# Two norm chains after memory attention, emitted between the gates of the second half-step

## The chip, the cores and the metric

The kernel runs on one core of one Trainium2 chip, in float32 throughout (matrix products take each operand as a high and a low float32r part). The metric is the device time of one execution in microseconds, the median of repeated runs. Before the change it was 2316.18 us (3 runs, 2313.41 to 2321.45).

## What is computed

One step of a one-layer decoder for 1,024 prompt tokens and 8 x 4 sample tokens, 1,056 tokens in all, of width 1024. The part that matters here is the end of the layer:

```python
c = memory_attend(rms_norm(h, p['xa_pre_g']), mem_k, mem_v, p['w_mem_q'], p['w_mem_o'])
h = h + rms_norm(c, p['xa_post_g'])
h = h + 0.5 * rms_norm(swiglu(rms_norm(h, p['ffn2_pre_g']), p['ffn2_w_gate'], p['ffn2_w_up'],
                              p['ffn2_w_down']), p['ffn2_post_g'])

def rms_norm(x, g):
    y = x * lax.rsqrt(jnp.mean(x * x, axis=-1, keepdims=True) + RMS_EPS)
    return y * g

def swiglu(x, w_gate, w_up, w_down):
    return (jax.nn.silu(x @ w_gate) * (x @ w_up)) @ w_down
```

`w_mem_o` is 1024 x 1024, the gate and up weights are 1024 x 2816, the down weight is 2816 x 1024.

## The kernel before

**Tiles.** The tokens are cut into three microbatches of 352 columns, t = 0, 1 and 2. An activation lies as 8 chunks of 128 features by 352 tokens. The high and low parts that TensorE reads are the tiles `X`; the raw activations lie in four large buffers, `K0` to `K3`. A product of 128 x 128 weights with 352 tokens is three matmuls (high by high, high by low, low by high, in `mm3`, L106).

**Weights.** Each block of 128 x 1024 weights is loaded by SyncE's queue into one of two `raw` buffers (L93), copied to its high part by ScalarE (L100) and subtracted into its low part by VectorE (L101). Six `w` buffers hold the split blocks, so three gates' worth of gate and up weights.

**The stage around the change.** `project(a["w_mem_o"], ...)` multiplies the attention output by `w_mem_o`, for t = 0, then 1, then 2, eight chunks of 24 matmuls each, and after each microbatch calls `after_o`. ScalarE empties each finished bank into the microbatch's `K` buffer (L1247). `after_o` then runs two norms on that buffer:

- `postnorm`: squares of the eight chunks (ScalarE, L115) are added up (VectorE, L117), one TensorE matmul with ones sums over the features (L164, into a bank `px`), VectorE takes the reciprocal root (L165, then L126 to L134), scales each chunk (L220) and adds the residual (L221). The residual comes chunk by chunk from DRAM (L1255) into two small buffers in `K1`, so chunk k+2 is not loaded before chunk k is added. The sum is stored to DRAM from ScalarE's queue (L1392, 1408 KB).
- for t = 1 and t = 2, `norm_in_place`: once more squares, sums, a matmul with ones and the reciprocal root, then eight products (L396), over the same buffer. For t = 0 it is `prenorm`, which writes `X` tiles.

**The gates.** Then 22 calls of `gate_up` run the gate and up products of t = 0 alone ("lone gates"): 24 matmuls into a gate bank and 24 into an up bank, VectorE scales the gate (L233), ScalarE takes the silu (L234), VectorE multiplies by the up bank (L235), and ScalarE's queue stores the product `sg` to DRAM (L236). There are six banks, so three gates, and two `sg` buffers. Microbatches 1 and 2 enter TensorE only after the gates and the down product of t = 0: `pair_operands` (L287 and on) reads both normed buffers and works on both at once.

**What sets the order.** The code is written in a sequence; a scheduler turns it into one fixed instruction list per engine, and gives earlier written work the higher priority. On the chip each engine walks its own list in order, and an instruction that waits holds up those behind it. DMA issues stand in the lists of SyncE and ScalarE.

Of the kernel before, what the change touches and what calls it, by code (L numbers as in the profile page):

```python
# [28 lines left out]
def decoder_step(tc, a, o):  # L29
# [18 lines left out]
    def R(tag, shape, bufs=1, dtype=F32, p=None):  # L48
        return (p or rp[0]).tile(list(shape), dtype, name=tag, tag=tag, bufs=bufs)

    def K(i):
        return kp_.tile([128, 2816], F32, name=f"K{i}", tag=f"K{i}", bufs=1)

    def K8(i):
        return K(i).rearrange("p (k n) -> p k n", n=NT)
# [12 lines left out]
    def bank():  # L68
        turn.append(turn.pop(0))
        return turn[-1].tile([128, 512], F32, name="mm", tag="mm", bufs=turn.count(turn[-1]))  # L70
# [19 lines left out]
    def stage(src, raw=None, width=1024):  # L90
        if raw is None:
            raw = wp.tile([128, 1024], F32, name="raw", tag="raw", bufs=2)[:, :width]
        sy.dma_start(raw, src)  # L93
        return raw

    def loadw(src, raw=None, width=1024):
        if raw is None:
            raw = stage(src, width=width)
        w = wp.tile([128, 2, 1024], F32R, name="w", tag="w", bufs=6)[:, :, :width]
        sc.activation(w[:, 0], raw, AF.Copy)  # L100
        v.tensor_sub(w[:, 1], raw, w[:, 0].bitcast(F32))  # L101
        return w

    def mm3(p, w, col, x, k, first, last, n=NT):
        for i, (wa, xa) in enumerate(PASSES):
            pe.matmul(p, w[:, wa, col:col + 128], x[xa][:, k, :n],  # L106
                      start=first and i == 0, stop=last and i == 2)
# [101 lines left out]
    def prenorm(t, h, gi, wide=False):  # L209
        hi, lo, tot = X(t), X(t), total()  # L210
        for k in range(8):
            half(hi, lo, h, gi, k)
            addsq(tot, h[:, k], k == 0)
        return hi, lo, (rstd_wide if wide else rstd)(tot, tag="rs", bufs=3)

    def postnorm(y, gi, resid, wide=False, last=False):
        ch = [y[:, k] for k in range(8)]
        rs = rstd_last(ch) if last else (rstd_wide if wide else rstd)(sqsum(ch))
        for k in range(8):
            v.scalar_tensor_tensor(y[:, k], y[:, k], gain(gi, k), rs, op0=ALU.mult, op1=ALU.mult)  # L220
            v.tensor_add(y[:, k], resid(k), y[:, k])  # L221
# [5 lines left out]
    def gate_up(x, w, out):  # L227
        pg, pu = bank(), bank()
        for p, ww in ((pg, w[0]), (pu, w[1])):
            for k in range(8):  # L230
                mm3(p[:, :NT], ww, k * 128, x, k, k == 0, k == 7)
        s = R("sg", [128, NT], 2)
        v.tensor_mul(s, pg[:, :NT], x[2])  # L233
        sc.activation(s, s, AF.Silu)  # L234
        v.tensor_mul(s, s, pu[:, :NT])  # L235
        sc.dma_start(out, s)  # L236

    def down(wd, h, y, parts, rs=None, filler=lambda: None):
        for c0, n in parts:
            p = [bank() if c < 6 else pbank() for c in range(n)]  # L240
            for k in range(0, NH, 2):
                x = R("raw2", [128, 1024], 2)[:, :2 * NT].rearrange("p (k n) -> p k n", k=2)
                hid = hidden(2)
                sy.dma_start(x, h[:, k:k + 2])
                split(x, hid[:, :, 0], hid[:, :, 1])
                if n == 8:
                    ws = [loadw(wd[k + j]) for j in range(2)]
                else:
                    raw = wp.tile([128, 1024], F32, name="raw", tag="raw", bufs=2)
                    for j in range(2):  # L250
                        sy.dma_start(raw[:, 512 * j:512 * j + 512], wd[k + j][:, c0 * 128:c0 * 128 + 512])
                    w = loadw(None, raw)
                    ws = [w[:, :, 0:512], w[:, :, 512:1024]]
                for j in range(2):
                    for c in range(n):
                        for q, (wa, xa) in enumerate(PASSES):
                            pe.matmul(p[c][:, :NT], ws[j][:, wa, c * 128:c * 128 + 128], hid[:, j, xa],  # L257
                                      start=k + j == 0 and q == 0, stop=k + j == NH - 1 and q == 2)
                    filler()
            for c in range(n):  # L260
                if rs is not None:
                    v.tensor_mul(y[:, c0 + c], p[c][:, :NT], rs)  # L262
                elif c % 2:
                    v.tensor_copy(y[:, c0 + c], p[c][:, :NT])
                else:
                    sc.activation(y[:, c0 + c], p[c][:, :NT], AF.Copy)
# [126 lines left out]
    def norm_in_place(y, gi):  # L393
        rs = rstd_wide(sqsum([y[:, k] for k in range(8)]))
        for k in range(8):
            v.scalar_tensor_tensor(y[:, k], y[:, k], gain(gi, k), rs, op0=ALU.mult, op1=ALU.mult)  # L396
# [384 lines left out]
    y = K8(ta)  # L781
# [17 lines left out]
    for i, t in enumerate((tb, tc_)):  # L799
        y = K8((tc_, tb)[i])  # L800
# [433 lines left out]
    def project(src, xs, order, done, before=lambda t: None, filler=lambda: None, ks=range(8)):  # L1234
        res = [loadw(src[c]) for c in range(4)]
        for t in order:
            before(t)
            y = K8(ys.pop(0))
            for c in range(8):
                w = res[c] if c < 4 else loadw(src[c])  # L1240
                p = bank()
                for k in ks:
                    mm3(p[:, :NT], w, k * 128, xs[t], k, k == ks[0], k == ks[-1])
                if len(xs[t]) == 3:
                    v.tensor_mul(y[:, c], p[:, :NT], xs[t][2])
                else:
                    sc.activation(y[:, c], p[:, :NT], AF.Copy)  # L1247
                filler()
            done(t, y)

    def resid(src):
        def get(k):
            hcs.append(hcs.pop(0))
            x = hcs[-1]
            sy.dma_start(x, src[:, k])  # L1255
            return x
        return get
# [129 lines left out]
        while t == 2 and next(sample[0], 0) is None:  # L1387
            pass

    def after_o(t, y):  # L1390
        postnorm(y, G_XA_POST, resid(hd[1][t]), True)
        sc.dma_start(hd[2][t], y)  # L1392
        if t == 0:
            xn[t] = prenorm(t, y, G_FFN2_PRE, True)
            return
        norm_in_place(y, G_FFN2_PRE)
        xn[t] = y

    project(a["w_mem_o"], cx, (0, 1, 2), after_o, drain, step)


# [16 lines left out]
    h2 = [scratch(f"h2_{t}", [128, NH, NT]) for t in range(3)]  # L1418
    for j in range(NH):
        gate_up(xn[0], (loadw(a["wg2"][j]), loadw(a["wu2"][j])), h2[2][:, j])  # L1420
    y = K8(3)
    down(a["wd2"], h2[2], y, ((0, 8),), xn[0][2])
    finish2(0, y)
# [4 lines left out]
    for i, parts in ((0, ((0, 8),)), (1, ((0, 4), (4, 4)))):  # L1428
        y = K8((3, 2)[i])
# [128 lines left out]
```

## Time and profile before

| | before |
|---|---|
| median of three runs | 2316.18 us |
| the profiled execution's own time | 2323.28 us |
| its span in the profile | 2321.5 us |
| TensorE busy with matmuls | 2233.3 us, 96% |
| VectorE busy | 1606.6 us, 69% |
| ScalarE busy | 987.1 us, 43% |
| mean granted TensorE clock | 0.981 |

The span is one execution as the hardware profiler saw it; the 1.8 us between it and the execution's own time lie outside the first and last instruction. "Busy" is the time in which an engine had an instruction running. TensorE's is the one engine near its limit, so a microsecond counts only where TensorE stands still, or runs at a lower clock. The profile's row of granted clock shows the latter: 1.00 is full speed.

### The profile page before, as it was taken

The numbers are of one execution on the slowest core, as the hardware profiler recorded it, in microseconds if no ns is written. First come the engines' busy times: TensorE is split into PE (matmuls) and PEld (weight loads), VectorE is DVE, ScalarE is ACT, GpSimd is POOL, SyncE is SP. The second block draws the span as 40 slices with busy tenths as digits, with TensorE's granted clock in tenths as the row PEclk, the third lists the DMA queues.
The fourth block names the chain that finished last, engine by engine and source line by source line (L and its number), as shares of the span: only waits on it lengthen the run. The fifth ranks groups of instructions, "written<-read, shape, count | busy, mean of one in ns | idle before, by whom it ended". The sixth has DMA issues, their size and how long they took to land.

```text
span 2321.5 us, 36671 instructions
## 1 busy us (share of the span) xinstructions
PE 2233.3 (96%) x14141; PEld 2137.7 (92%) x14141; DVE 1606.6 (69%) x3357; ACT 987.1 (43%) x1784; POOL 9.7 (0%) x22
## 2 busy tenths in 40 slices
PE   8999999999999999999899999995999999999997
PEld 8999999999999998887899789895999999999997
DVE  8986778897557658688668654687446676665474
ACT  5434345554445314356544223442334444444352
POOL 0000000000000000000000000000000000000000
PEclk9999999999999999999899999997999999999998
DMA  7567545455667323443145631454556343335673
GB/s 259 175 186 206 171 126 170 136 167 160 205 186 239 122 62 125 143 144 97 46 138 159 241 110 54 159 177 145 176 162 201 95 147 108 119 98 189 186 221 110
DMA packets 151278, 355.23 MB, mean 153 GB/s; under 512 B 17952, under 2 KB 68384, under 8 KB 149664
## 3 DMA queue, kind: packets, MB, share of 16 engines
q1 hardware_dynamic: 99712, 294.30, 41.3%
q10 hardware_dynamic: 51392, 58.59, 7.3%
q8 instruction: 111, 1.82, 0.3%
q14 instruction: 63, 0.52, 0.1%
HBM read 296.35 MB, written 59.59 MB: 153 GB/s over the span
## 4 chain that ended last, share of the span: by engine, by line
PE 81%; DVE 8%; DMA 7%; ACT 2%; issue 1%; ACTq 1%; SPq 0%; DVEq 0%
PE mm L106 26%; PE mm L333 21%; PE mm L257 14%; PE px L106 3%; PE px L257 3%; DMA sp<-K 1%; PE cs L1290 1%; DVE K L497 1%; PE cv L1315 1%; DVE w L101 1%; PE px L1212 1%; PE ac L913 1%; DVE K L220 1%; PE px L478 1%; DVE K L221 1%
## 5 line engine op out<-in xcount | busy, mean ns | idle before, releaser
L106 PE MATMUL mm<-X,w 128*128 128x352 f32 x4272 | 711.5, 326 | 12.1 <-ACT X L196 6.3
L106 PEld LDWEIGHTS mm<-X,w 128*128 128x128 f32 x4272 | 689.1, 189 | 26.7 <-issue 9.0
L100 ACT ACTIVATE w<-raw 128x1024 fp32r<-128x1024 f32 x293 | 309.1, 1056 | 387.9 <-PE mm L106 112.6
L101 DVE TENSOR_TENSOR w<-raw,w 128x1024 fp32r<-128x1024 f32 x293 | 358.3, 1223 | 163.8 <-ACT w L100 161.1
L257 PE MATMUL mm<-hid,w 128*128 128x352 f32 x2640 | 455.2, 327 | 13.8 <-DVE hid L185 7.5
L257 PEld LDWEIGHTS mm<-hid,w 128*128 128x128 f32 x2640 | 432.6, 189 | 18.2 <-DVE hid L185 10.3
L333 PE MATMUL mm<-xq,w 128*128 128x352 f32 x2112 | 364.5, 323 | 1.9 <-DVE K L262 1.3
L333 PEld LDWEIGHTS mm<-xq,w 128*128 128x128 f32 x2112 | 341.7, 188 | 4.3 <-DVE K L262 1.6
L313 DVE TENSOR_TENSOR w<-raw,w 128x512 fp32r<-128x512 f32 x308 | 202.8, 686 | 48.1 <-ACT w L312 47.0
L312 ACT ACTIVATE w<-raw 128x512 fp32r<-128x512 f32 x308 | 180.1, 624 | 119.4 <-PE mm L333 36.2
L333 PE MATMUL mm<-X,w 128*128 128x352 f32 x1056 | 186.6, 323 | 2.1 <-ACT q L347 2.1
L333 PEld LDWEIGHTS mm<-X,w 128*128 128x128 f32 x1056 | 171.2, 188 | 4.7 <-ACT q L347 3.2
L185 DVE TENSOR_TENSOR hid<-raw,hid 128x704 fp32r<-128x704 f32 x88 | 78.2, 890 | 92.3 <-ACT hid L184 87.2
L184 ACT ACTIVATE hid<-raw 128x704 fp32r<-128x704 f32 x88 | 69.5, 789 | 142.9 <-PE px L257 59.2
L497 DVE TENSOR_TENSOR K<-K 128x256 f32<-128x256 f32 (+4 forms) x380 | 105.8, 318 | 25.0 <-DMA sp<-K 12.4
L257 PE MATMUL px<-hid,w 128*128 128x352 f32 x528 | 101.9, 327 | 0.0
L117 DVE TENSOR_TENSOR tot<-tot,sq 128x352 f32<-128x352 f32 x179 | 93.1, 520 | 10.8 <-ACT sq L115 8.4
L115 ACT ACTIVATE sq<-K 128x352 f32<-128x352 f32 x170 | 80.8, 489 | 42.1 <-DVE tot L117 24.7
L333 PE MATMUL mm<-K,w 128*128 128x352 f32 x528 | 97.6, 325 | 0.0
L257 PEld LDWEIGHTS px<-hid,w 128*128 128x128 f32 x528 | 89.6, 190 | 0.0
L333 PEld LDWEIGHTS mm<-K,w 128*128 128x128 f32 x528 | 87.0, 188 | 1.1 <-issue 1.1
L1247 ACT ACTIVATE K<-mm 128x352 f32<-128x352 f32 x48 | 22.3, 465 | 86.4 <-PE mm L106 86.1
(328 smaller groups left out, 2192.2 us busy)
## 6 DMA issues: line engine op xcount, KB each, us to landing
raw<-wd SPq DMA_DIRECT2D x88, 512.0 KB
raw<-wu SPq DMA_DIRECT2D x87, 512.0 KB
raw<-wg SPq DMA_DIRECT2D x86, 512.0 KB
raw<-h SPq DMA_DIRECT2D x88, 352.0 KB
raw<-wd SPq DMA_DIRECT2D x88, 256.0 KB
h<-hid ACTq DMA_DIRECT2D x44, 352.0 KB
sp<-sp SPq DMA_DIRECT2D x16, 848.0 KB
h<-K ACTq DMA_DIRECT2D x9, 1408.0 KB
```

What stands on the lines that cost most here:

```text
L100: sc.activation(w[:, 0], raw, AF.Copy)
L101: v.tensor_sub(w[:, 1], raw, w[:, 0].bitcast(F32))
L106: pe.matmul(p, w[:, wa, col:col + 128], x[xa][:, k, :n], start=first and i == 0, stop=last and i == 2)
L115: sc.activation(q, c, AF.Square)
L117: eng.tensor_add(tot, tot, q)
L184: sc.activation(hi, x, AF.Copy)
L185: v.tensor_sub(lo, x, hi.bitcast(F32))
L257: pe.matmul(p[c][:, :NT], ws[j][:, wa, c * 128:c * 128 + 128], hid[:, j, xa], start=k + j == 0 and q == 0, stop=k + j == NH - 1 and q == 2)
L312: sc.activation(w[:, 0], x, AF.Copy)
L313: v.tensor_sub(w[:, 1], x, w[:, 0].bitcast(F32))
L333: pe.matmul(p, w[a_][:, wa, k * 128:k * 128 + 128], x[b_][xa][:, k], start=start and k == 0 and i == 0, stop=k == 3 and i == 2, skip_group ...
L497: v.tensor_tensor(out, x, y, op)
```

## The change

`after_o` keeps the norms of t = 0 where they were. For t = 1 and t = 2 it only remembers the microbatch, and the same two norms, now in `last_norm`, are called after gate 1 (for t = 1) and after gate 3 (for t = 2) of the 22 lone gates. No operation is added or left out; the lists differ in order only.

```diff
-    def after_o(t, y):
+    def last_norm(t, y):
         postnorm(y, G_XA_POST, resid(hd[1][t]), True)
         sc.dma_start(hd[2][t], y)
         if t == 0:
...
             return
         norm_in_place(y, G_FFN2_PRE)
         xn[t] = y
+
+    rest = []
+
+    def after_o(t, y):
+        if t == 0:
+            last_norm(t, y)
+        else:
+            rest.append((t, y))
 
     project(a["w_mem_o"], cx, (0, 1, 2), after_o, drain, step)
 
@@ -1418,6 +1426,8 @@
     h2 = [scratch(f"h2_{t}", [128, NH, NT]) for t in range(3)]
     for j in range(NH):
         gate_up(xn[0], (loadw(a["wg2"][j]), loadw(a["wu2"][j])), h2[2][:, j])
+        if j in (1, 3):
+            last_norm(*rest[j // 2])
     y = K8(3)
```

What it does to the lists is seen best on VectorE. In the list before, at the end of the second norm of t = 2 (`K_15049` is its buffer, `K_11753` is `K1` with the residual); the two L233 rows are those of gates 2 and 3, and the L235 row is that of gate 2:

```order
L221 TENSOR_TENSOR K_15049<-K_11753,K_15049 128x352 x2
L117 TENSOR_TENSOR tot<-tot,sq 128x352 x2
L165 TENSOR_SCALAR tot<-px 128x352
L126 TENSOR_SCALAR y<-tot 128x352
L127 SCALAR_TENSOR_TENSOR sq<-y 128x352
L128 TENSOR_TENSOR sq<-sq,tot 128x352
L129 SCALAR_TENSOR_TENSOR y<-sq,y 128x352
L233 TENSOR_TENSOR sg<-mm,rs 128x352
L130 TENSOR_TENSOR sq<-y 128x352
L233 TENSOR_TENSOR sg<-mm,rs 128x352
L131 TENSOR_TENSOR sq<-sq,tot 128x352
L235 TENSOR_TENSOR sg<-sg,mm 128x352
```

In the changed list the same gate 2 stands inside the first norm of t = 1, which begins with the L165 row; the first L235 row is that of gate 1, the L233 and the last L235 are those of gate 2:

```order
L235 TENSOR_TENSOR sg<-sg,mm 128x352
L165 TENSOR_SCALAR tot<-px 128x352
L101 TENSOR_TENSOR w<-raw,w 128x1024
L126 TENSOR_SCALAR y<-tot 128x352
L127 SCALAR_TENSOR_TENSOR sq<-y 128x352
L128 TENSOR_TENSOR sq<-sq,tot 128x352
L129 SCALAR_TENSOR_TENSOR y<-sq,y 128x352
L233 TENSOR_TENSOR sg<-mm,rs 128x352
L130 TENSOR_TENSOR sq<-y 128x352
L101 TENSOR_TENSOR w<-raw,w 128x1024
L131 TENSOR_TENSOR sq<-sq,tot 128x352
L185 TENSOR_TENSOR hid<-raw_16835,hid 128x2x352
```

Gate 2's rows have moved from behind the norms of both microbatches to ahead of nearly all of them, and from there on the L233, L235 and L101 rows of one gate after another alternate with the rows of the norms, up to gate 15.

On TensorE the matmuls with ones move. In the list before, these are the last two of them, `px_15301` (first norm of t = 2) and `px_15363` (its second); `mm_15667` is the up bank of gate 4, `mm_15731` the gate bank of gate 5, and `X0` the operand of t = 0:

```order
L164 MATMUL px_15301<-tot_15278,ones_96 128x352
L106 MATMUL mm_15667<-X0_14601,w_15663 128x352 x2
L106 MATMUL mm_15667<-X0_14602,w_15663 128x352
L106 MATMUL mm_15667<-X0_14601,w_15663 128x352 x2
L106 MATMUL mm_15667<-X0_14602,w_15663 128x352
L106 MATMUL mm_15667<-X0_14601,w_15663 128x352
L164 MATMUL px_15363<-tot_15340,ones_96 128x352
L106 MATMUL mm_15731<-X0_14601,w_15723 128x352
```

In the changed list the first matmul with ones of t = 1 stands at the end of gate 1, and its second is this one, `px_15397`, inside the up bank of gate 6 (`mm_15797`):

```order
L106 MATMUL mm_15797<-X0_14601,w_15793 128x352 x2
L106 MATMUL mm_15797<-X0_14602,w_15793 128x352
L164 MATMUL px_15397<-tot_15374,ones_96 128x352
L106 MATMUL mm_15797<-X0_14601,w_15793 128x352 x2
L106 MATMUL mm_15797<-X0_14602,w_15793 128x352
```

Where 7 gate matmuls stood between the two sums of t = 2, the changed list has 221 between those of t = 1, and 210 between those of t = 2 (from gate 9 to gate 14).

SyncE's list decides when the residual chunks are loaded. In the list before, the last six of t = 2 (`h_2`) stand together behind all weights loaded so far:

```order
L93 DMA raw<-wu 128x1024
L1255 DMA K_11753<-h_2_134 128x352 x6
L244 DMA raw_16835<-h_2_15395 128x704
```

In the changed list those of t = 1 (`h_1`) go in pairs between weight loads and a first load for the down product (L244):

```order
L1255 DMA K_11753<-h_1_133 128x352 x2
L93 DMA raw<-wg 128x1024
L93 DMA raw<-wu 128x1024
L1255 DMA K_11753<-h_1_133 128x352 x2
L93 DMA raw<-wg 128x1024
L244 DMA raw_16898<-h_2_15181 128x704
L1255 DMA K_11753<-h_1_133 128x352 x2
L93 DMA raw<-wu 128x1024
```

A pair now waits its turn behind up to two blocks of weights, and the weights behind a pair wait until two chunks have been added. On ScalarE the stores of gates 0 and 1 (L236), which stood behind the 1408 KB store of t = 2 (L1392), now follow right on their silu. Behind the last gate all lists are as they were.

## The prediction

> **What bounds the kernel now.** I read the page first: the row of busy tenths by slice (58 us each) and the row of the granted clock.
>
> ```profile
> PE   8999999999999999999899999995999999999997
> PEclk9999999999999999999899999997999999999998
> ```
>
> TensorE is full nearly everywhere. One slice stands out, the 28th (1567 to 1625 us): busy 5, clock 7. So next the busy time by stretches around it; the columns are length, then the busy time (and instructions) of each engine, the granted clock, the DMA share and GB/s.
>
> ```profile
> 1538.60:1578.50 39.90, 39.90 (x246) 39.18 (x245) 30.57 (x53) 18.63 (x27) 0.00 (x0) 1.00 0.63 205
> 1578.50:1605.40 26.90, 1.54 (x2) 0.53 (x3) 19.94 (x40) 5.13 (x10) 0.00 (x0) 0.59 0.44 147
> 1605.40:1620.00 14.60, 14.59 (x76) 14.60 (x77) 12.90 (x24) 5.25 (x8) 0.00 (x0) 0.82 0.39 98
> 1620.00:1740.00 120.00, 120.00 (x752) 120.00 (x751) 55.21 (x64) 40.61 (x49) 0.00 (x0) 1.00 0.57 173
> ```
>
> Before and behind the hole TensorE has no gap. In the hole VectorE works 19.94 of 26.90 us. TensorE's timeline says who ended the hole:
>
> ```profile
> 1554.12 22.67 PE L106 MATMUL mm<-X,w 128*128 128x352 f32 x139
> 1576.63 0.75 PE L164 MATMUL px<-tot,ones 128*128 128x352 f32 x2
> 1576.95 1.55 PE L106 MATMUL mm<-X,w 128*128 128x352 f32 x7
> 1599.97 1.54 PE L164 MATMUL px<-tot,ones 128*128 128x352 f32 x2 [21.47 <-DVE tot L117]
> 1605.41 133.18 PE L106 MATMUL mm<-X,w 128*128 128x352 f32 x816 [3.90 <-DVE sg L233]
> ```
>
> After the seven matmuls of gate 4 TensorE stands 21.47 us before the last matmul with ones (second norm of t = 2): its operand needs the whole first norm. Then 3.90 us more for a free bank, which L233 of gate 2 must empty. VectorE's and ScalarE's timelines show why gate 2 is so late:
>
> ```profile
> 1555.03 0.51 DVE L235 TENSOR_TENSOR sg<-sg,mm 128x352 f32<-128x352 f32 x1
> ...
> 1599.39 0.53 DVE L117 TENSOR_TENSOR tot<-tot,sq 128x352 f32<-128x352 f32 x1 [0.50 <-ACT sq L115]
> ...
> 1604.74 0.52 DVE L233 TENSOR_TENSOR sg<-mm,rs 128x352 f32<-128x352 f32 x1 [0.60 <-DMA h<-sg]
> ```
>
> ```profile
> 1598.49 0.33 ACTq L1392 DMA_DIRECT2D h<-K  x1
> ...
> 1598.89 1.39 ACTq L236 DMA_DIRECT2D h<-sg  x2
> ```
>
> No gate is evicted from 1555.03 (end of gate 1) to 1604.74: the rest of both norms stands ahead in VectorE's list. The stores of gates 0 and 1, which free the two `sg` buffers, are issued behind the big store at 1598.49. What ends last is thus the chain of t = 2, with gates 2 to 4 full behind it.
>
> **The change, part by part.** *The hole goes.* TensorE stops at 1578.50 and resumes at 1605.41: 26.91 us. The matmul with ones in it remains and costs, at full speed, what the spacing of ScalarE's evictions in `project` shows:
>
> ```profile
> 1519.16 0.47 ACT L1247 ACTIVATE K<-mm 128x352 f32<-128x352 f32 x1 [1.66 <-PE mm L106]
> ...
> 1523.59 0.47 ACT L1247 ACTIVATE K<-mm 128x352 f32<-128x352 f32 x1 [3.02 <-PE mm L106]
> ...
> 1527.43 0.47 ACT L1247 ACTIVATE K<-mm 128x352 f32<-128x352 f32 x1 [2.43 <-PE mm L106]
> ```
>
> A chunk of 24 matmuls takes 3.84 us (1523.59 to 1527.43), so 0.160 us each and 7.68 us a gate; with a matmul with ones in it 4.43 us, so that one costs 0.59 us. Removed: 26.91 - 0.59 = 26.3 us.
>
> *The clock stays up.* Behind the hole the clock comes back late:
>
> ```profile
> 1608.00:1610.00 2.00, 2.00 (x9) 2.00 (x8) 1.51 (x4) 0.79 (x1) 0.00 (x0) 0.50 0.45 159
> 1610.00:1612.00 2.00, 2.00 (x12) 2.00 (x11) 2.00 (x6) 0.00 (x0) 0.00 (x0) 0.85 0.33 62
> 1612.00:1614.00 2.00, 2.00 (x15) 2.00 (x14) 2.00 (x5) 0.76 (x2) 0.00 (x0) 1.00 0.30 118
> ```
>
> The 816 matmuls of gates 5 to 21 run from 1605.41 to 1738.42, where the down product's first matmul starts:
>
> ```profile
> 1738.42 2.59 PE L257 MATMUL mm<-hid,w 128*128 128x352 f32 x15
> ```
>
> That is 133.0 us; at 0.160 us they take 130.6. Without the hole 2.4 us more go.
>
> The Trainium skill ("TensorE: Matmul & The Clock Gate", Part 1) says that the array's clock falls to half after an idle window of about 3.4 us and comes back after about 3.4 us of sustained work. The granted 0.50 agrees, but it lasts here from 1605.41 to beyond 1610, some 5 us. By the Trainium skill's 3.4 us at half speed this term would be an estimated 1.7 us and the sum 28.0 us. I go by the rows.
>
> *The norms move into the gates.* Every operation remains: per microbatch two roots of 10 steps, 8 L220, 8 L221, 7 + 7 L117 and 8 L396 on VectorE, the squares on ScalarE, two matmuls with ones, eight residual loads on SyncE and a store on ScalarE's queue, of these sizes:
>
> ```profile
> h<-K ACTq DMA_DIRECT2D x2, 1408.0 KB
> K<-h SPq DMA_DIRECT2D x14, 176.0 KB
> ```
>
> The matmuls with ones are paid before and after. The rest lies beside TensorE's work if two things hold: VectorE keeps the gates fed, and each sum is ready when TensorE reaches its matmul with ones. In the steady gates VectorE is busy 55.21 of 120 us, so 4.1 of 7.68 us a gate are free. Two chains from the end of gate 1 to about gate 16 are 15 gates, so 62 us free. How long the parts take when VectorE runs without waiting:
>
> ```profile
> 1563.79 0.53 DVE L133 TENSOR_TENSOR sq<-sq,tot 128x352 f32<-128x352 f32 x1
> 1564.23 0.52 DVE L117 TENSOR_TENSOR tot<-tot,sq 128x352 f32<-128x352 f32 x1
> 1564.67 0.52 DVE L134 SCALAR_TENSOR_TENSOR y<-sq,y 128x352 f32<-128x352 f32 x1
> 1565.10 1.22 DVE L101 TENSOR_TENSOR w<-raw,w 128x1024 fp32r<-128x1024 f32 x1
> 1566.24 4.05 DVE L396 SCALAR_TENSOR_TENSOR K<-K,c_gains,y 128x352 f32<-128x352 f32 x8
> ```
>
> So 0.44 us for a small operation, 1.14 for a weight split, 4.0 for eight products; the root's steps need each other's results, and I take 0.5 for each. A microbatch is 20 x 0.5 + 22 x 0.44 + 2 x 4.0 = 27.7 us, two are 55 of 62 us. It fits, with little to spare.
>
> *The second sum.* From the first matmul with ones of t = 1 to its second TensorE has 221 matmuls, 35.4 us. VectorE's list has between them the root steps (10 x 0.5), L220 (4.0), 23 rows of L221, L117, L233 and L235 (10.1), 8 weight splits (9.1) and two L185 for the down product (some 1.6, taken at 0.8): 29.8 us. For t = 2 it is 210 matmuls, 33.6 us, against 5.0 + 4.0 + 10.1 + 7 splits at 1.14 = 27.1 us. What VectorE waited in the chain inside the hole:
>
> ```profile
> L221 DVE TENSOR_TENSOR K<-K,K 128x352 f32<-128x352 f32 x8 | 4.1, 524 | 2.8 <-DMA K<-h 2.8
> ...
> L117 DVE TENSOR_TENSOR tot<-tot,sq 128x352 f32<-128x352 f32 x7 | 3.7, 522 | 1.5 <-ACT sq L115 1.5
> ```
>
> That is 4.3 us, which leaves 1.3 us for t = 1 and 2.2 us for t = 2. A new wait on TensorE can cost nothing, or, with late residual loads, the sums of the rivals below; a gain below nothing is excluded, since TensorE has no gap in the gates (120.00 of 120.00 us). The nearest row is the chain of t = 1 as it runs before, with loads and splits interleaved and TensorE not waiting:
>
> ```profile
> 1522.60:1553.80 31.20, 31.20 (x196) 31.07 (x195) 26.48 (x44) 16.68 (x26) 0.00 (x0) 1.00 0.65 203
> ```
>
> There 193 matmuls were enough for the same chain. I take nothing.
>
> *Queues.* SyncE's 16 loads and the two stores are 16 x 176 + 2 x 1408 KB = 5.6 MB, over 15 gates (115 us) some 50 GB/s on top of 173, so about 220 GB/s, near the 203 and 205 GB/s at which TensorE had no gap. On SyncE a pair of residual loads that waits for VectorE holds the weight loads behind it, but the splits run about two gates (15 us) ahead of use. On ScalarE's queue the store of gate 5 stands behind the 1408 KB store of t = 1. In the hole such a store took 5.8 us (1598.89 to 1604.74); L233 of gate 7, which needs its buffer, comes 1.5 gates or 11.5 us later, which hides it.
>
> *What is late next.* Nothing needs the normed buffers before L287, at 1739 us:
>
> ```profile
> 1609.93 4.05 DVE L396 SCALAR_TENSOR_TENSOR K<-K,c_gains,y 128x352 f32<-128x352 f32 x8
> ...
> 1739.13 1.62 DVE L287 TENSOR_TENSOR xq<-K 128x1408 f32<-128x1408 f32 x1
> ```
>
> L396 of t = 2 ended 125 us ahead of it. In the changed list it stands behind gate 14, so some 50 us ahead. That cover is enough.
>
> **Sum:** 26.3 + 2.4 = 28.7 us. The profiled execution's own time was 2323.3 us (span 2321.5 and 1.8 around it), so it would become 2294.6. That execution lies 7.1 us above the median of 2316.2 and above all three timed runs; no view says where those 7.1 us lie, so I take the 28.7 us from the median: 2287.5 us.
>
> **The rivals.** *A wait on the sum takes the hole's place.* Against it are the spare 1.3 and 2.2 us; for it, that residual loads now stand behind weights on SyncE. The chain of what ended last shows both kinds:
>
> ```profile
> 1538.25 5.31 DMA K<-h
> ...
> 1550.12 7.67 DMA raw<-wu
> ...
> 1589.08 2.94 DMA K<-h
> ...
> 1592.66 2.39 DMA K<-h
> ...
> 1595.63 2.28 DMA K<-h
> ```
>
> In the hole a pair took 2.5 us on average; among weights 5.31 was seen. If all three pairs of a chain took that, it would be 8.3 us later: TensorE waits 8.3 - 1.3 = 7.0 and 8.3 - 2.2 = 6.1 us, and loses twice 2.4 us of clock. 28.7 - 17.9 = 10.8 us remain: 2305.4 us.
>
> By the Trainium skill's rule above, waits shorter than about 3.4 us would cost no clock; none of that length stands in a row here.
>
> *VectorE starves TensorE (slower than before).* L221 waits in VectorE's list ahead of splits and evictions of later gates. If each pair took as long as the slowest weight load in those rows, 7.67 us, each chain would be 15.4 us later, as much as the splits' lead of two gates, and TensorE would stop at every pair: 15.4 - 1.3 and 15.4 - 2.2 are 27.3 us, and six stops at 2.4 us of clock 14.4 more. That is 41.7 us lost against 28.7 gained: 2316.2 + 13.0 = 2329.2 us. With six stops the loss passes the gain from about 5.5 us a pair (6 x 3.0 more than now, less the spare 3.5, plus 14.4, is 28.9). Against it: the longest wait seen for a pair is 5.31 us, and one of that length alone, in which the lead of two gates isn't eaten.
>
> *The change doesn't move what binds.* If gate 2 were held by something else than the list, the hole would remain: 2316 us. Against it: the rows of VectorE name the list and the store, and both have moved.
>
> **How the numbers follow.** Forecast (no new wait, or up to 5 us of them) 0.80; wait on the sum of 5 to 18 us 0.13; hole remains or is eaten up 0.04; starving 0.03. The range reaches 6 us below the forecast (the three runs before span 8 us) and up to just under the first rival's full price, 2281 to 2304 us; some 1 in 10 is left out. A measurement can tell about 0.3% (7 us) from no change. Faster by more: the forecast and nearly all of the first rival, 0.93; within: 0.04; slower: 0.03.
>
> **What would show it.** In the profile of the changed kernel TensorE's gates run from `project` to the down product in 22 x 7.68 + 4 x 0.59 = 171.3 us, against 199.8 now (from 1538.60, where the first stretch above begins, to 1738.42). The granted clock is 1.00 throughout; no L164 waits over 1 us for L117; L233 of gate 2 comes about 20 us after the first gate matmul. The step on the clock is wrong if 816 matmuls still take over 131 us; the step on the second sum if L164 shows a wait for L117; the step on the lead if L106 waits for L101 or L233. The prediction fails if a residual pair takes over 5 us among the weights.

## The result, and the profile after

| | before | changed |
|---|---|---|
| median | 2316.36 us (4 runs, 2313.41 to 2321.45) | 2292.54 us (4 runs, 2291.27 to 2294.98) |
| ratio | | 0.9896, 95% interval 0.9876 to 0.9916 |
| span of the profiled execution | 2321.5 us | 2289.5 us |
| mean granted TensorE clock | 0.981 | 0.989 |

The change saves 23.8 us, about 1.0%. The forecast was 28.7 us and 2287.5 us, with a range of 2281 to 2304. One of the five executions of run 10 below took 2429.32 us at a granted clock of 0.847; the ratio given there leaves it out, and the median would be 2294.06 us without it. Below, "the stage" is the stretch from the 0.78 us wait early in the `w_mem_o` product of t = 2 to the first matmul of the down product. It holds the matmuls of `w_mem_o` for t = 2 but for the first two, and those of all 22 gates: 190 + 1,056 = 1,246. It is cut at the same wait in every run but the seventh (the wait itself is 0.89 us in run 3 and 1.62 to 1.63 us in runs 5, 6 and 8).

The page's rows of busy tenths and of the clock, for the changed kernel:

```profile
PE   8999999999999999999899989999999999999997
PEclk9999999999999999999899999999999999999998
```

The 5 and the 7 of the 28th slice are gone. TensorE's timeline of the changed kernel (start, length, what, and in brackets the idle time before it with what ended it):

```profile
1503.38 46.08 PE L106 MATMUL mm<-X,w 128*128 128x352 f32 x286 [0.78 <-DVE X L1369]
1549.30 0.75 PE L164 MATMUL px<-tot,ones 128*128 128x352 f32 x2
1549.62 35.79 PE L106 MATMUL mm<-X,w 128*128 128x352 f32 x221
1585.25 0.76 PE L164 MATMUL px<-tot,ones 128*128 128x352 f32 x2
1585.58 24.31 PE L106 MATMUL mm<-X,w 128*128 128x352 f32 x149
1609.72 0.75 PE L164 MATMUL px<-tot,ones 128*128 128x352 f32 x2
1610.05 34.03 PE L106 MATMUL mm<-X,w 128*128 128x352 f32 x210
1645.70 0.86 PE L164 MATMUL px<-tot,ones 128*128 128x352 f32 x2 [1.62 <-DVE tot L117]
1646.13 61.23 PE L106 MATMUL mm<-X,w 128*128 128x352 f32 x380
1707.20 2.59 PE L257 MATMUL mm<-hid,w 128*128 128x352 f32 x15
```

One wait is left, 1.62 us before the second sum of t = 2. The stage takes 203.8 us (1503.38 to 1707.20). Before, it began here:

```profile
1507.59 14.89 PE L106 MATMUL mm<-X,w 128*128 128x352 f32 x91 [0.78 <-DVE X L1369]
```

That is 230.8 us to 1738.42, so 27.0 us less now. The rest of the 32 us between the two spans is spread: the stage starts 4.2 us earlier in this execution, though nothing ahead of it differs between the kernels, and what follows it takes 582.3 instead of 583.1 us. Busy time by stretches of the changed kernel (columns as in the prediction):

```profile
1536.60:1578.50 41.90, 41.90 (x262) 41.69 (x261) 31.71 (x52) 18.82 (x25) 0.00 (x0) 1.00 0.56 183
1578.50:1660.00 81.50, 79.88 (x495) 78.95 (x493) 65.64 (x114) 33.14 (x48) 0.00 (x0) 1.00 0.68 218
1660.00:1707.00 47.00, 47.00 (x295) 47.00 (x295) 25.18 (x33) 16.01 (x20) 0.00 (x0) 1.00 0.56 170
```

The clock is 1.00 in all three, and DMA runs at up to 218 GB/s, about the 220 that was worked out.

### The profile page after: what moved, and what is told of

Read it like the earlier page. It is cut to its first block, busy times and chain, and to the rows that moved or that the text cites. A ratio compares the mean times of both kernels' runs of the same rounds, so it can differ in the third digit from the quotient of the medians.

```text
span 2289.5 us, 36667 instructions
## 1 busy us (share of the span) xinstructions
PE 2227.0 (97%) x14141; PEld 2132.3 (93%) x14141; DVE 1601.4 (70%) x3357; ACT 986.9 (43%) x1784; POOL 9.7 (0%) x22
## 4 chain that ended last, share of the span: by engine, by line
PE 81%; DVE 7%; DMA 6%; ACT 2%; issue 2%; ACTq 1%; SPq 0%; DVEq 0%
PE mm L106 25%; PE mm L333 23%; PE mm L257 15%; PE px L257 3%; PE px L106 3%; DMA sp<-K 2%; PE cv L1315 1%; DVE K L497 1%; PE cs L1290 1%; DVE w L101 1%; PE ac L913 1%; PE px L478 1%; DVE K L220 1%; PE px L1212 1%; DMA raw<-wd 1%
## 5 line engine op out<-in xcount | busy, mean ns | idle before, releaser
L106 PE MATMUL mm<-X,w 128*128 128x352 f32 x4272 | 709.4, 325 | 8.3 <-ACT X L196 6.3
L106 PEld LDWEIGHTS mm<-X,w 128*128 128x128 f32 x4272 | 686.7, 189 | 22.2 <-ACT X L196 6.6
L101 DVE TENSOR_TENSOR w<-raw,w 128x1024 fp32r<-128x1024 f32 x293 | 357.8, 1222 | 178.9 <-ACT w L100 176.0
L100 ACT ACTIVATE w<-raw 128x1024 fp32r<-128x1024 f32 x293 | 309.1, 1056 | 372.2 <-PE mm L106 84.8
L497 DVE TENSOR_TENSOR K<-K 128x256 f32<-128x256 f32 (+4 forms) x380 | 105.4, 317 | 31.5 <-DMA sp<-K 14.3
L117 DVE TENSOR_TENSOR tot<-tot,sq 128x352 f32<-128x352 f32 x179 | 92.7, 518 | 7.3 <-ACT sq L115 4.9
```

Of the source, the lines that this page charges most:

```text
L106: pe.matmul(p, w[:, wa, col:col + 128], x[xa][:, k, :n], start=first and i == 0, stop=last and i == 2)
L117: eng.tensor_add(tot, tot, q)
L497: v.tensor_tensor(out, x, y, op)
```

## The experiments

Two yardsticks help. By the prediction's durations a stage without a stop takes 1,246 x 0.160 + 4 x 0.59 = 201.7 us. And the stage, read from one profile, separates kernels better than the whole time: the executions of one kernel spread over up to 14 us (2310.68 to 2325.02 for the kernel before, measured beside runs 1 to 4).

**1 and 2. Both kernels again.** No edit.

> The kernel before, unchanged, once more. Theory A (the hole is fixed by the instruction lists, and what differs between executions lies elsewhere): TensorE stands between gate 4 and gate 5 for 25.5 to 28 us again, and the stage from the first w_mem_o matmul of t = 2 to the down product takes 229 to 232 us (230.8 in the first profile). Rival R (the hole depends on how the residual loads fall, and the first profile showed a long one): the hole is 20 to 24 us. Both: ratio 1.000 within 0.002.

> The changed kernel, unchanged, once more. Theory A: the same stage takes 203 to 205 us (203.8 in the first profile), one wait of 0.5 to 3 us before the last matmul with ones, ratio 0.988 to 0.990 (27.0 us of stage gone from 2316). Rival R: the stage as in A, but the ratio is 0.990 to 0.992, since the hole that goes is shorter in most executions.

Measured: 2319.01 us (ratio 1.0009, interval 0.9997 to 1.0021) and 2291.58 us (ratio 0.9904, 0.9889 to 0.9919). The kernel before, TensorE's timeline:

```profile
1600.69 1.54 PE L164 MATMUL px<-tot,ones 128*128 128x352 f32 x2 [20.79 <-DVE tot L117]
1606.14 133.22 PE L106 MATMUL mm<-X,w 128*128 128x352 f32 x816 [3.91 <-DVE sg L233]
```

The hole is 26.2 us (26.9 in the first profile), the 816 matmuls behind it take 133.1 us again, the stage 230.2 us. The changed kernel's stage takes 202.9 us with a wait of 0.69 us. So rival R falls: the hole belongs to the lists. Both profiles of the kernel before come from executions 6 to 7 us above their medians (2323.28 against 2316.36, 2325.45 against 2319.01), and no trace shows the hole of a median one; run 4 speaks for the full hole there too, as its median gained as much as its stage. The changed kernel's ratio alone could not have told the two apart, as its interval covers the figures of both.

**3 and 4. One microbatch alone.** In 3 only t = 1 is put off, in 4 only t = 2:

```diff
-        if t == 0:
+        if t != 1:          # run 4: if t != 2:
             last_norm(t, y)
...
-        if j in (1, 3):
-            last_norm(*rest[j // 2])
+        if j == 1:          # run 4: if j == 3:
+            last_norm(*rest[0])
```

> Only the norms of t = 1 are emitted behind gate 1; those of t = 2 stay where they were, ahead of the gates. Theory A (the hole is two chains back to back in VectorE's list, longer than the three gates that the banks hold; one chain alone is shorter than that): no hole over 3 us, time 2290 to 2298 us, ratio 0.988 to 0.992. Rival H (each chain brings its own half of the hole): 2304 us, ratio 0.995. Rival T (the norm of t = 2 alone makes the hole, as TensorE waited for its sum): 2312 us or more, ratio 0.998 to 1.000.

> Only the norms of t = 2 are emitted behind gate 3; those of t = 1 stay where they were. Theory A: no hole over 3 us, 2290 to 2296 us, ratio 0.988 to 0.991. Rival H: 2304 us, ratio 0.995. Rival T: 2290 to 2296 us.

Measured: 2296.37 us (0.9919, 0.9906 to 0.9931) and 2288.65 us (0.9882, 0.9868 to 0.9896). TensorE's timeline of run 3, then of run 4 from the second sum of t = 1 on:

```profile
1570.49 0.75 PE L164 MATMUL px<-tot,ones 128*128 128x352 f32 x2
1576.45 30.86 PE L106 MATMUL mm<-X,w 128*128 128x352 f32 x175 [4.41 <-DVE sg L233]
...
1710.92 2.59 PE L257 MATMUL mm<-hid,w 128*128 128x352 f32 x15
```

```profile
1553.32 0.75 PE L164 MATMUL px<-tot,ones 128*128 128x352 f32 x2
1579.20 0.76 PE L164 MATMUL px<-tot,ones 128*128 128x352 f32 x2
1613.23 0.76 PE L164 MATMUL px<-tot,ones 128*128 128x352 f32 x2
1709.06 2.59 PE L257 MATMUL mm<-hid,w 128*128 128x352 f32 x15
```

Rivals H and T fall: putting off either microbatch takes away most of the hole, so it is neither half and half nor the chain of t = 2 alone. In run 3 one chain still stands ahead of gate 2's L233, and TensorE stops 4.41 us; theory A had allowed 3. In run 4 nothing stops it, and the stage is 201.9 us, the yardstick within 0.2.

**5. The kernel before, residual loaded at once into K1.**

```diff
     def after_o(t, y):
-        postnorm(y, G_XA_POST, resid(hd[1][t]), True)
+        x = load_x(1, hd[1][t])
+        postnorm(y, G_XA_POST, lambda k: x[:, k], True)
```

> The kernel before, with the residual of a microbatch loaded into all of K1 at once (four DMAs of 352 KB) instead of chunk by chunk into two small buffers; both norms still stand ahead of the gates. Theory A (the hole is the work of two chains standing back to back in VectorE's list): only VectorE's 4.3 us of waiting in the hole go, the hole is 18 to 24 us instead of 26.9, ratio 0.996 to 0.999. Rival L (the hole is the landing of the residual loads, two at a time): hole under 10 us, ratio 0.991 to 0.994.

Measured: 2315.35 us (0.9983, 0.9971 to 0.9995). The end of its hole, which begins at 1576.8 us, on TensorE:

```profile
1591.12 1.54 PE L164 MATMUL px<-tot,ones 128*128 128x352 f32 x2 [14.31 <-DVE tot L117]
1593.80 132.62 PE L106 MATMUL mm<-X,w 128*128 128x352 f32 x816 [1.14 <-DVE sg L233]
```

The hole is 17.0 us, 1 us under the range of theory A and far above rival L's. But not for the reason given: between the two sums of t = 2 this execution takes 25.0 us (1566.13 to 1591.12), not less than the 23.3 before. It is the chain of t = 1 that is shorter (27.8 against 31.5 us), so that of t = 2 starts earlier against the gates. Of the 9.9 us that the hole is shorter, some 3 are lost again where the stage begins: its first 42 matmuls take 9.8 us instead of 6.7, most of them at a clock of 0.50 (run 6 shows the same). The stage is 223.3 us, 7.5 less than in the first profile. This profile is of the fastest of ten executions (2310.07 us); the medians differ by 3.1 us. Loading residuals early eases the hole; two chains ahead of the gates remain.

**6. The changed kernel, residual loaded at once.** The same edit in `last_norm`; here as in run 5 it reaches t = 0 too.

> The changed kernel, with the residual loaded into all of K1 at once. Theory A (what is left of the wait on the second sum of t = 2 comes from the residual loads and weight splits among which its chain runs): no wait of TensorE for L117 over 0.5 us, the stage from w_mem_o of t = 2 to the down product 202 to 203 us (203.8 and 202.9 with chunks), ratio 0.987 to 0.990. Rival B (1408 KB in a lump hold up the weight loads behind them on SyncE): waits of L106 for L101 of 2 us or more, stage 205 us or more.

Measured: 2296.53 us (0.9902, 0.9880 to 0.9924), no wait for L117, none of L106 for L101. The stage takes 205.0 us. That is too long for theory A, and it meets rival B's length without rival B's waits, so the reason is a third one: 3 us of it lie in its first 46 matmuls. First TensorE's timeline, then the clock (the first of the last three numbers):

```profile
1509.96 0.44 PE L1365 MATMUL sw<-c_ident,q 128*128 128x128 f32 x2 [0.55 <-DVE q L1362]
1510.77 0.58 PE L106 MATMUL mm<-X,w 128*128 128x352 f32 x2 [0.37 <-ACT X L1368]
1512.98 10.78 PE L106 MATMUL mm<-X,w 128*128 128x352 f32 x46 [1.63 <-DVE X L1369]
```

```profile
1512.00:1514.00 2.00, 1.02 (x3) 1.02 (x4) 2.00 (x5) 0.66 (x2) 0.00 (x0) 0.64 0.52 119
1516.00:1518.00 2.00, 2.00 (x9) 2.00 (x8) 1.93 (x6) 0.99 (x2) 0.00 (x0) 0.50 0.52 209
1520.00:1522.00 2.00, 2.00 (x15) 2.00 (x14) 0.00 (x0) 1.41 (x2) 0.00 (x0) 1.00 0.00 0
```

Three short waits, 2.55 us in all, lie within 4 us, and behind them the clock is at half for some 6 us. In the changed kernel the L1365 matmuls had no wait and that before the stage was 0.78 us, at a clock of 1.00; runs 5 and 8, with the same edit, begin like run 6. In the gates themselves each piece has the length of the yardstick.

**7. One small residual buffer instead of two,** in all three microbatches.

```diff
-    hcs = [k1[:, 2048 + NT * i:2048 + NT * i + NT] for i in range(2)]
+    hcs = [k1[:, 2048 + NT * i:2048 + NT * i + NT] for i in range(1)]
```

> The changed kernel with one small residual buffer instead of two, in all three microbatches: every residual load now waits for the chunk before it. This prices late residual loads. Theory W (lateness reaches TensorE only at the matmuls with ones): in the gates TensorE waits at L164 for L117, 0 to 8 us each, and at no L106 for L101 or L233; 2291 to 2310 us. Rival S (VectorE starves the gates): L106 waits for L101 or L233 several times, 2315 us or more.

Measured: 2317.99 us (0.9997, 0.9983 to 1.0010), beyond theory W's range. What TensorE waited for over the whole execution (us, times, longest):

```profile
PE sw L1339 <- DMA kv<-mem_kT: 9.2, 6, 2.9
...
PE sw L1339 <- DMA kv<-mem_v: 8.2, 6, 4.5
PE px L164 <- DVE tot L117: 4.1, 2, 3.1
```

Most of the time is lost ahead of the gates, whose first matmul comes some 22 us later than in the changed kernel: waits of L1339 (memory attention of the sample group) come to 17.4 us, against 3.3 in the changed kernel, because the edit touches t = 0 too and shifts the whole list. In the gates W holds: two waits for L117, 1.02 and 3.12 us, and none of L106 for L101 or L233. As the scheduler also spaced the sums wider (292 and 279 matmuls instead of 221 and 210), this is no clean price of a late load.

**8. Run 4 with the residual loaded at once.**

> Only the norms of t = 2 moved behind gate 3, as in the run that moved them alone (2288.65 us), and the residual loaded into all of K1 at once. Theory A: nothing is left to gain in this stage (it already ran at 201.9 us, TensorE without a wait), so the same time within the spread: 2285 to 2292 us, ratio 0.987 to 0.9895. Rival L (residual loads still cost somewhere in the stage): 2284 us or less.

Measured: 2296.35 us (0.9896, 0.9879 to 0.9914), slower than expected by either. The stage takes 204.9 us, with no wait for L117 and the same half clock at its beginning as in run 6. That explains 3 of the 7.7 us between the medians of runs 4 and 8; the two were measured on different chips, and the intervals of their ratios overlap. Loading at once has nothing to give in the gates, and the stage begins worse.

**9 to 11. Run 4 and the changed kernel again, and the norms of t = 2 much later.** Run 11 is the changed kernel with

```diff
-        if j in (1, 3):
-            last_norm(*rest[j // 2])
+        if j in (1, 15):
+            last_norm(*rest[j // 15])
```

> The kernel with only the norms of t = 2 moved, once more beside the changed kernel. Theory A (its stage has no wait left, the changed kernel's has 0.7 to 1.8 us): the stage takes 201.5 to 202.5 us, and its time is 1 to 3 us below that of the changed kernel on the same chip: 2286 to 2292 us, ratio 0.987 to 0.990. Rival E (the two are equal, the first difference was spread between executions): within 1 us of each other.

> The changed kernel a third time, as the neighbour of the run before it. Theory A: stage 202.7 to 204 us, 2290 to 2295 us, ratio 0.988 to 0.991. Rival E: as the run before it, within 1 us.

> The changed kernel with the norms of t = 2 emitted behind gate 15 instead of gate 3, so that the two chains no longer follow on each other and the last products L396 stand beside gate 21, right ahead of L287. Theory A (the wait on the second sum of t = 2 comes from weight splits that are late behind the first chain): no wait of L164 for L117 over 0.5 us, stage 201.9 to 202.5 us, same time as the changed kernel or up to 2 us less. Rival C (the normed buffers are then needed at once, the 50 us of cover are gone): the down product or the first pair product waits 5 us or more, and the time is 2296 us or more.

Measured: 2289.25 us (0.9876, 0.9862 to 0.9889), 2294.31 us (0.9890, 0.9872 to 0.9908) and 2290.08 us (0.9883, 0.9867 to 0.9899). The stage takes 201.9, 204.2 and 201.9 us. In run 11 the products L396 now end right ahead of L287; VectorE's timeline:

```profile
1702.99 4.05 DVE L396 SCALAR_TENSOR_TENSOR K<-K,c_gains,y 128x352 f32<-128x352 f32 x8
...
1709.66 1.62 DVE L287 TENSOR_TENSOR xq<-K 128x1408 f32<-128x1408 f32 x1
```

From the down product's start to 1834 us TensorE never waits there, so rival C falls: the buffers may be ready as late as that, since the down product of t = 0 still stands between. Theory A holds for the wait and the stage: with the chains apart, the last wait is gone. The median is 4.2 us below the changed kernel's, where 2 at most was expected. The runs speak against rival E, with 5.1 us between 9 and 10 where the stage explains 2.2, but the intervals overlap. Run 4's kernel has the lowest medians, 2288.65 and 2289.25 us, against 2292.54, 2291.58 and 2294.31 for the changed kernel; run 11's 2290.08 can't be told from them.

## Why the prediction was right

- **The hole.** Shown. It was to give 26.3 us; both profiles before have it (26.9 and 26.2 us), none of the changed kernel does, and each chain taken out of the way alone closes most of it. Its mechanism, as put, was gates held in VectorE's list behind two chains. Run 3 bears on it most directly: one chain ahead of gate 2's L233 leaves a stop of 4.41 us, and it is L233 that ends it.
- **The clock.** Shown. 816 matmuls took 133.0 and 133.1 us before; now gates run at 0.160 us a matmul and the clock is 1.00. The Trainium skill's rule ("TensorE: Matmul & The Clock Gate", Part 1) had given an estimated 1.7 us; the traces measure 2.4. Even the short stop of run 3 cost its share: the stage is 209.1 us, 7.4 over the yardstick, of which 4.41 are the stop.
- **The norms beside the gates.** Right: wherever the norms of t = 2 are put off, no gate waits for L101 or L233. No row speaks for the starving rival.
- **The second sum.** Here the sum was mis-sized. For t = 1 a spare of 1.3 us was given; its last L117 ends at 1584.39 and TensorE comes at 1585.25, so 0.9 us. For t = 2 it was 2.2 us, and TensorE waited 1.62 (0.69 and 1.67 in the other profiles of this kernel). The step took it that VectorE turns to the sum as soon as TensorE has it. VectorE's and ScalarE's timelines of the changed kernel show what came first:

```profile
1610.88 1.23 DVE L101 TENSOR_TENSOR w<-raw,w 128x1024 fp32r<-128x1024 f32 x1 [1.99 <-ACT w L100]
...
1614.41 1.23 DVE L101 TENSOR_TENSOR w<-raw,w 128x1024 fp32r<-128x1024 f32 x1 [1.86 <-ACT w L100]
1615.55 0.52 DVE L165 TENSOR_SCALAR tot<-px 128x352 f32<-128x352 f32 x1
```

```profile
1609.79 1.06 ACT L100 ACTIVATE w<-raw 128x1024 fp32r<-128x1024 f32 x1 [2.79 <-DMA raw<-wu]
1613.32 1.06 ACT L100 ACTIVATE w<-raw 128x1024 fp32r<-128x1024 f32 x1 [2.46 <-DMA raw<-wg]
```

TensorE begins the sum at 1609.72; L165 runs at 1615.55, 5.8 us later, behind two splits whose weights had not landed. From the first matmul with ones to its L165 it had been 0.8 us for t = 1 and 1.3 us for t = 2 in the kernel before. Behind L165 the chain waited 3.1 us in all, less than the 4.3 us that were allowed. With the 27.1 us of rows that makes 5.8 + 27.1 + 3.1 = 36.0 us, against some 34.4 us of TensorE's work between the two sums. So the term at fault is this delay of 5.8 us, which was taken as nothing. A wait on the sum had been named as a rival and priced for late residual loads; this one came from late weight loads ahead in the list, and it was small. The delay is 0.8 us in run 11, where the chains stand apart, and 3.1 us in run 4, and neither has the wait. That the loads were late because of the first chain's own place on SyncE was not tried by itself.
- **The rivals' price.** Too high. The prediction was to fail if a residual pair took over 5 us among the weights. In the chain that ended last two pairs of t = 1 did, 5.33 us from 1568.70 and 5.17 us from 1574.99, and the forecast held. VectorE waited for them once:

```profile
1580.18 0.53 DVE L221 TENSOR_TENSOR K<-K,K 128x352 f32<-128x352 f32 x1 [2.04 <-DMA K<-h]
```

Splits and gate rows stood between in its list and filled the rest of the time. The rivals counted all that a pair takes beyond 2.5 us as lateness of the chain; here two long pairs cost 2.04 us, less than the 2.8 us that the old chain waited for its residuals. Of the other signs, the one against the sum's step came (a wait for L117 over 1 us), those against the clock and the lead did not.
- **The whole time.** 28.7 us less the wait of 1.6 is 27.1 us, and the stage gained 27.0. The medians gained 23.8, 25.5 and 22.6 us in three comparisons. Some 3 us are thus missing in the medians. Ahead of the stage and behind it the profiles show no steady difference: the stage starts at 1507.6 and 1509.0 us before, at 1503.4, 1510.1 and 1508.5 after. For run 4's kernel medians and stage agree (28.4 and 27.7 against 28.6 us, from the mean of the two stages before). It is the width of the range, and not the sum, that covers these 3 us. Whether the second sum waits longer in executions without a profile stays open.
- **Cover ahead of L287.** Right and more than needed: run 11 takes it to about 3 us without a loss.

## What to carry to other kernels

Where an engine walks a fixed list, look at a hole's end for the first instruction that was ready early and stood behind a long chain; what matters is whether the work queued ahead is longer than the buffers can hold, not how busy the engine is. Move only as much as closes the hole: the second of the two chains was enough, and its stage was 1 to 2 us shorter than with both moved close behind each other; moved far apart, both did as well. The first alone left a stop of 4.41 us. When pricing a moved chain, start counting at the instruction's own place in the list, with the waits of everything ahead of it there.

## What was not expected of the hardware

The clock falls after shorter stops than the 26.9 us hole suggested, and it takes about as long to return. After the 4.41 us stop of run 3 it was 0.50 until 1582 us, 5.5 us after TensorE had resumed:

```profile
1576.00:1578.00 2.00, 1.55 (x5) 1.58 (x6) 1.97 (x6) 1.66 (x3) 0.00 (x0) 0.50 0.36 146
1580.00:1582.00 2.00, 2.00 (x9) 2.00 (x8) 2.00 (x5) 0.00 (x0) 0.00 (x0) 0.50 0.45 86
1582.00:1584.00 2.00, 2.00 (x14) 2.00 (x13) 0.16 (x1) 0.81 (x1) 0.00 (x0) 0.95 0.56 221
```

In run 6 the clock fell likewise behind three waits of 0.55, 0.37 and 1.63 us, while the single 1.62 us wait of the changed kernel left it at 1.00. So short waits close together can cost 3 us that the view of the waits doesn't show. The length of the waits alone doesn't decide it: a single one of 1.99 us in run 6, ended at 1498.19 us, was followed by 0.50 from 1499 to 1502 us, and one of 2.02 us in run 8, ended at 1492.24 us, left 1.00. Nor is the return always as late: in run 7 the clock was back 3.1 us after the stop of 3.12 us had ended. Read in windows of half a microsecond, the stretches at half clock last 3.4 us (run 7, the first of run 6), 6.8 us (run 3, the second of run 6) or 27.3 us (in and behind the hole of the kernel before), all whole multiples of 3.4 us. What a stop costs thus seems to depend also on how it falls into such steps. The Trainium skill ("TensorE: Matmul & The Clock Gate", Part 1) puts the fall at an idle window of about 3.4 us; run 6 has no idle time of that length ahead of these two falls, and there the measurement decides.
